# A hybrid decoder step on one Trainium2 core: low parts of the values' weights by VectorE alone, and an end in a written order that leaves GpSimd out

## The chip, the core and the metric

The kernel runs on one core of a Trainium2 chip. The core's engines work side by side, each through its own queue in order: TensorE (PE; its weight loads are shown as PEld), VectorE (DVE), ScalarE (ACT), GpSimd (POOL) and SyncE (SP), which here only starts DMAs. GpSimd and ScalarE can start DMAs too. [...] An engine waits for another by a semaphore. The metric is the device time of one execution in microseconds (us), less is better.

## What is computed

The reference is one layer of a decoder for 512 prompt tokens and 64 sample tokens (8 sequences of 8), 1024 wide, all in fp32. Cut to what matters here:

```python
def hybrid_layer(x, ...):
    u = _rms(x) * g_pre_mix
    proj = u @ w_in                       # z, xbc, dt, q, k, v, gates, og
    ...
    y_ssd = ssd_scan(...)                 # Mamba-2 heads, with carried states
    h_ml = mlstm_scan(q, k, v, ...)       # v: 4 heads of 256
    x = x + _rms(mix) * g_post_mix
    ...                                   # cross attention on a memory, the same frame
    u = _rms(x) * g_pre_ffn
    f = (silu(u @ w_gate) * (u @ w_up)) @ w_down
    x = x + _rms(f) * g_post_ffn
    return x, ...
```

The change touches the weights of v within the first projection, and everything from the last part of `@ w_down` for the first 256 tokens on: the sum of squares of f, its root, the residual, and the store of x.

## The kernel before

Activations are kept with features on the 128 partitions and the 576 tokens along the free axis, in 8 tiles. Tokens are worked in two parts, HALVES: 0 to 255 and 256 to 575.

**Products in two parts.** A weight of fp32 is split into a high part hi (fp32r, a cast on ScalarE) and a low part lo = raw - hi; activations likewise. A product is three matmuls: hi by hi, hi by the activation's low part, lo by hi (`gemm`, L201 to L203). `split_w` (L173 to L189) loads a unit of 128 x 1024 weights into one of two `raw` buffers, casts it into one of three `whi` buffers, and makes `wlo` in two pieces: columns 0 to cut on VectorE (L188), the rest either on GpSimd or, with `acc`, by ScalarE writing -hi (L185) and a DMA from GpSimd's queue that adds the weights from HBM onto it (L186).

**Values.** `gemm_tok` (L756) makes v for one head with the tokens on the partitions: two units of weights, `units[0]` for the first four feature tiles and `units[1]` for the other four. For every 128 tokens it runs 4 x 3 matmuls of 256 columns with the first unit, then 4 x 3 with the second (L775 to L777); for the 64 sample tokens, two forms of matmul per feature tile (L767, L768). L793 calls it for the four heads with `acc`, cut at column 512. The memory's values use the same function without `acc`. This stage lies among the state updates of the SSD scan, which run on GpSimd (L589, L597, L633, L725) and VectorE (L598, L611, L614, L729).

**Order.** Most of the kernel is ordered by a planner, which simulates the program with its own durations and so fixes the order on each engine; `tc.issue_after` adds an edge. From the cross attention's output projection to the gated products the order is written by hand: `at_(p, fn, ...)` puts a step at place p of `plan`, and the steps are issued sorted by p inside `tc.manual_schedule`, for the engines named there.

**The end.** The down projection's last 6 feature tiles are added for tokens 256 to 575 first (`down_chunk`), then for tokens 0 to 255, j = 0 to 7: 18 matmuls each (`down_part`), then `down_evac` (L1860): VectorE adds PSUM onto f2 (L1863), ScalarE squares (L262, L266), VectorE adds the square onto `ssqf` (L267), ScalarE scales f2 by the gain (L1865). Between these, for tokens 256 to 575, come the root (`rstd_cols`, `newton`: sums over partitions by matmul with ones, L226; mean on VectorE, L236; power -0.5 on GpSimd, L237; one Newton step on VectorE, L238 to L240), its rows by transposes (L251) copied by ScalarE (L253), and the residual (`post_add`, VectorE, L1038, L1039) with four stores of 320 KB from SyncE (L1918). `x2` holds x, loaded back from DRAM. Where an order is not written it is the planner's.

`final0` then does tokens 0 to 255, which leave with tokens on the partitions, in four quarters `parts`: 4 transposes of x2 per quarter (L1876) and a copy to SBUF on ScalarE (L1884), the root of `ssqf`, 4 transposes of f2 per quarter, and quarter 0, 1 and 3 on VectorE (L1898: f2 by the root plus x); quarter 2 is scaled on ScalarE (L1895) and added on GpSimd (L1896). SyncE issues the four stores of 256 KB (L1899). PE's order is written here: three quarters of x, the sums of the root, the fourth, then f2. L2020 is the closing of the program: each engine drains, and GpSimd collects and releases the barrier.

Of the kernel before, what the change touches and what calls it, by code (L numbers as in the profile page):

```python
# [116 lines left out]
def build(nc, tc, ctx, I, O):  # L117
# [27 lines left out]
    def B0(name):  # L145
        return pn[0].tile([P, 512], F32, name=name, tag="n0")
# [26 lines left out]
    def split_w(src, n=1024, cut=CUT, acc=False, pool=None, to=None, raw=None):  # L173
        if raw is None:
            raw = wp.tile([P, 1024], F32, name="raw", tag="raw", bufs=2)
        loads.append(S.dma_start(raw[:, :n], src))
        if to:
            split(*to, raw[:, :n])
            return to
        hi, lo = [(pool or wp).tile([P, 1024], F32R, name=k, tag=k, bufs=NWX if pool else 3) for k in ("whi", "wlo")]  # L180
        A.copy(hi[:, :n], raw[:, :n])  # L181
        for e, a, b in ((V, 0, cut), (G, cut, n)):
            if b > a and e is G and acc:

                A.activation(lo[:, a:b], hi[:, a:b].bitcast(F32), AF.Copy, scale=-1.0)  # L185
                G.dma_start(lo[:, a:b], src[:, a:b], accum_op=ALU.add)  # L186
            elif b > a:
                e.tensor_tensor(lo[:, a:b], raw[:, a:b], hi[:, a:b].bitcast(F32), op=ALU.subtract)  # L188
        return hi, lo  # L189
# [30 lines left out]
    def rstd_cols(ssq, chunks, name, d=1024.0, alloc=None):  # L220

        nch = len(chunks)
        ps = (alloc or BP)("ps_ss")
        for j in range(nch):
            for i, t_ in enumerate(ssq):
                ssq_mm.append(mm(ps[:, j:j + 1], t_[:, chunks[j][0]:chunks[j][0] + P], ones, start=i == 0,  # L226
                                 stop=i == len(ssq) - 1, skip_group_check=True))
        return newton(ps[:, :nch], [P, nch], name, d)
# [524 lines left out]
        G.memset(v_[:, :, 256:257], 1.0)  # L753
        G.memset(v_[:, :, 257:258], 0.0)

    def gemm_tok(src, xh_, xl_, chunks, evac, acc=False, units=None):  # L756

        units = units or [split_w(src[:, i, :], acc=acc) for i in range(2)]
        for c0 in range(0, len(chunks), 2):
            ps = GP("ps_v")  # L760
            for c, (t0, n) in enumerate(chunks[c0:c0 + 2]):
                if n == TS:

                    for k in range(KT):
                        hi, lo = units[k // 4]
                        j = (k % 4) * 256
                        mm(ps[:, 0:256], xh_(k, t0, P), hi[:, j:j + 256], start=k == 0, stop=k == KT - 1, skip_group_check=True)  # L767
                        mm(ps[:n, 0:256], xh_(k, t0, n), lo[:, j:j + 256], start=False, stop=k == KT - 1, skip_group_check=True)  # L768
                    break
                for k in range(KT):  # L770
                    hi, lo = units[k // 4]
                    j = (k % 4) * 256
                    ah, al = xh_(k, t0, n), xl_(k, t0, n)
                    o = ps[:n, c * 256:c * 256 + 256]
                    mm(o, ah, hi[:, j:j + 256], start=k == 0, stop=False, skip_group_check=True)  # L775
                    mm(o, al, hi[:, j:j + 256], start=False, stop=False, skip_group_check=True)
                    m = mm(o, ah, lo[:, j:j + 256], start=False, stop=k == KT - 1, skip_group_check=True)  # L777
            evac(c0, ps)
        return m

    def v_evac(h):
        def ev(c, ps):
            if c < 4:
                for i in range(2):
                    A.activation(vt4[:, c + i, h, 0:256], ps[:, 256 * i:256 * i + 256], AF.Copy, scale=rx[:, c + i:c + i + 1])
            else:
                A.copy(vts[:TS, h, 0:256], ps[TS:P, 0:256])
                V.tensor_tensor(vts[:TS, h, 0:256], vts[:TS, h, 0:256], ps[:TS, 0:256], op=ALU.add)
                A.activation(vts[:TS, h, 0:256], vts[:TS, h, 0:256], AF.Copy, scale=rx[:TS, 4:5])
        return ev  # L790

    for h in range(4):
        gemm_tok(I["wv"][h], U, UL, CHUNKS, v_evac(h), True)  # L793


    st = ExitStack()
# [983 lines left out]
    def down_part(c, nk, j, i, ps, w, k0, k1):  # L1780
        t0, n = HALVES[i]
        return gemm(ps, [(*w, nk)], act(hh), act(hl), t0, n, k0, k1)
# [86 lines left out]
    with tc.issue_after(loads[-1].ins):  # L1869
        S.dma_start(x2, x_d)  # L1870

    def final0():

        def rows(src, c, d, ps):
            for j in range(4):
                m = TE.transpose(ps[:, j * P:(j + 1) * P], src[:, 4 * d + j, c * P:(c + 1) * P], ident)  # L1876
            return ps.rearrange("p (j k) -> p j k", j=4), m

        parts = [(c, d) for c in range(2) for d in range(2)]
        xr = [wp.tile([P, 2, 4, P], F32, name="raw", tag="raw", bufs=2) for _ in range(2)]  # L1880
        xt = [xr[i // 2][:, i % 2] for i in range(4)]

        def put(i):
            A.copy(xt[i], rows(x2, *parts[i], (B1 if i == 3 else GP)("ps_xt"))[0])  # L1884

        with tc.manual_schedule(engines={TE.engine}):
            for i in range(3):
                put(i)
            rc = rstd_cols([ssqf], HCHUNKS[0], "pf0", alloc=B0)
            put(3)  # L1890
            ft = [rows(f2, *parts[i], (GP if i == 3 else MP)("ps_ft"))[0] for i in range(4)]
        for i, (c, d) in enumerate(parts):
            if i == 2:
                t = sw[:, 0:512].rearrange("p (j k) -> p j k", j=4)
                A.activation(t, ft[i], AF.Copy, scale=rc[:, c:c + 1])  # L1895
                G.tensor_tensor(xt[i], xt[i], t, op=ALU.add)  # L1896
            else:
                V.scalar_tensor_tensor(xt[i], ft[i], rc[:, c:c + 1], xt[i], op0=ALU.mult, op1=ALU.add)  # L1898
            S.dma_start(O["y0"][c, :, 4 * d:4 * d + 4, :], xt[i])  # L1899


    for n_, j in enumerate(range(8)):
        ps = (MP if n_ % 2 else GP)("ps_dn")[:, :256]
        m = down_part(2, 6, j, 0, ps, w_of(j), 0, 6)
        e = down_evac(n_, j, 0, ps, m)
        if n_ == 0:
            with tc.issue_after(m.ins):
                rc = rstd_cols([ssqf], HCHUNKS[1], "pf1", alloc=B0)
        if n_ == 1:
            with tc.issue_after(m.ins):  # L1910
                rstd_rows(rc, HCHUNKS[1], rb, B0)
        if n_ > 1:
            ks = range(8)[:2] if n_ == 2 else range(8)[n_ - 1:n_] if n_ < 7 else range(6, 8)
            for k in ks:
                with tc.issue_after(e[1].ins):
                    post_add(1, f2, x2, rb, [k], False)
                if k % 2:
                    S.dma_start(O["y1"][:, k - 1:k + 1, :], x2[:, k - 1:k + 1, 256:T])  # L1918
    final0()


def _units(w, kt):
# [102 lines left out]
```

## Time and profile before

| what | value |
|---|---|
| median of 3 runs | 1122.03 us (1121.79 to 1123.79) |
| the profiled execution | 1122.92 us, its span 1121.2 us |
| granted TensorE clock, mean | 0.998 |
| DMA | 178.67 MB, mean 159 GB/s |
| of it from GpSimd's queue (q0) | 39.33 MB |
| loads of the values' weights | 8 x 512 KB, median 5.7 us to landing |
| accumulating DMAs of the values' low parts | 8 x 256 KB, median 6.8 us to landing |
| PE busy in 1107.5 to 1112.0 | 3.43 us of 4.5 |
| PE busy in 1112.0 to 1121.2 | 0.70 us of 9.2 |

The span runs from the first to the last instruction of the profiled execution; some 1.7 us of its time lie around it. Times within the trace count from the span's start. A busy PE is a modelled figure: matmuls overlap, so that a matmul of 256 columns is shown as 0.28 us while the next starts 0.12 us later. Drains and semaphore instructions belong to an engine's sequencer and are not counted as busy; they have rows of their own under the line that issued them.

### The profile page before, as it was taken

The page shows a single profiled execution, that of the slowest core. Times are in us where ns is not written, and L with a number is a line of the kernel's source. Part 1 is how long each engine was busy: PE and PEld are TensorE (multiplying, and loading weights), DVE is VectorE, ACT ScalarE, POOL GpSimd, SP SyncE. Part 2 cuts the span into 40 slices and gives each one's busy share as a digit, 9 for nine tenths or more (in the row PEclk, how much of TensorE's full clock was granted, in tenths as well). Part 3 has the DMA queues.
Part 4 walks back from the last instruction along what each step waited for, and adds up shares of the span by engine and source line. Part 5 has one row for each costly group of instructions (what it writes and reads, how often), then busy time and mean ns, then how long its engine had stood idle before and what let it go on. Part 6 is the DMA issues. An engine that isn't in the chain of part 4 may idle for free.

```text
span 1121.2 us, 21126 instructions
## 1 busy us (share of the span) xinstructions
PE 1100.6 (98%) x8423; PEld 1049.9 (94%) x8423; DVE 703.7 (63%) x1397; ACT 594.3 (53%) x1073; POOL 223.0 (20%) x300
## 2 busy tenths in 40 slices
PE   9999999899999999999999999999999999999996
PEld 8999889798998999999988889999999999999996
DVE  6796765557786775569654455776533665447555
ACT  6877533255563465656454445556435674246543
POOL 1333544313122121000144301101001110011001
PEclk9999999999999999999999999999999999999999
DMA  6685555626564447653567855745535774357532
GB/s 208 159 165 128 134 159 159 174 68 166 146 201 107 129 144 264 226 189 104 167 223 278 282 197 170 253 114 123 141 95 122 171 169 123 94 119 169 123 127 85
DMA packets 56231, 178.67 MB, mean 159 GB/s; under 512 B 6172, under 2 KB 10396, under 8 KB 55620
## 3 DMA queue, kind: packets, MB, share of 16 engines
q1 hardware_dynamic: 41732, 137.99, 37.8%
q0 software_dynamic: 14400, 39.33, 18.2%
q8 instruction: 66, 1.08, 0.4%
q14 instruction: 33, 0.27, 0.1%
HBM read 156.64 MB, written 20.65 MB: 158 GB/s over the span
## 4 chain that ended last, share of the span: by engine, by line
PE 89%; DMA 4%; DVE 2%; ACT 2%; issue 1%; POOL 1%; SPq 0%; DVEq 0%; POOLq 0%; ACTq 0%
PE ps_in L202 6%; PE ps_in L201 6%; PE ps_in L203 6%; PE ps_dn L203 4%; PE ps_dn L201 4%; PE ps_dn L202 4%; PE ps_o L203 3%; PE ps_o L202 3%; PE ps_o L201 3%; PE ps_g L1719 3%; PE ps_g L1720 3%; PE ps_g L1721 3%; PE ps_u L1719 3%; PE ps_u L1720 3%; PE ps_u L1721 3%; PE ps_v L777 2%
## 5 line engine op out<-in xcount | busy, mean ns | idle before, releaser
L181 ACT CAST whi<-raw 128x1024 fp32r<-128x1024 f32 x110 | 114.6, 1045 | 113.6 <-PE ps_dn L202 22.0
L202 PE MATMUL ps_in<-ul,whi 128*128 128x320 f32 (+1 forms) x544 | 164.3, 302 | 0.0
L201 PE MATMUL ps_in<-uh,whi 128*128 128x320 f32 (+1 forms) x544 | 163.9, 301 | 0.0
L203 PE MATMUL ps_in<-uh,wlo 128*128 128x320 f32 (+1 forms) x544 | 163.0, 300 | 0.5 <-DVE wlo L188 0.5
L188 DVE TENSOR_TENSOR wlo<-raw,whi 128x1024 fp32r<-128x1024 f32 (+1 forms) x102 | 102.8, 1009 | 82.0 <-ACT whi L181 81.2
L202 PEld LDWEIGHTS ps_in<-ul,whi 128*128 128x128 f32 x544 | 103.1, 190 | 2.5 <-issue 1.7
L201 PEld LDWEIGHTS ps_in<-uh,whi 128*128 128x128 f32 x544 | 103.1, 190 | 2.2 <-issue 1.3
L203 PEld LDWEIGHTS ps_in<-uh,wlo 128*128 128x128 f32 x544 | 103.1, 190 | 1.8 <-DVE wlo L188 0.7
L203 PE MATMUL ps_dn<-hh,wlo 128*128 128x320 f32 (+1 forms) x280 | 82.3, 296 | 0.8 <-DVE wlo L188 0.8
L201 PE MATMUL ps_dn<-hh,whi 128*128 128x320 f32 (+1 forms) x280 | 81.8, 296 | 0.6 <-ACT whi L181 0.5
L202 PE MATMUL ps_dn<-hl,whi 128*128 128x320 f32 (+1 forms) x280 | 82.0, 294 | 0.0
L203 PEld LDWEIGHTS ps_dn<-hh,wlo 128*128 128x128 f32 x280 | 52.5, 188 | 1.2 <-DVE wlo L188 1.2
L201 PEld LDWEIGHTS ps_dn<-hh,whi 128*128 128x128 f32 x280 | 52.3, 188 | 1.0 <-ACT whi L181 0.7
L202 PEld LDWEIGHTS ps_dn<-hl,whi 128*128 128x128 f32 x280 | 52.9, 189 | 0.0
L186 POOL DMA_DIRECT2D wlo<-win x32 | 27.9, 880 | 95.2 <-ACT wlo L185 89.2
L1719 PE MATMUL ps_u<-b,whi 128*128 128x288 f32 x144 | 42.5, 295 | 0.6 <-ACT ct L1751 0.6
L1720 PE MATMUL ps_u<-b,whi 128*128 128x288 f32 x144 | 42.5, 295 | 0.0
L1719 PE MATMUL ps_g<-b,whi 128*128 128x288 f32 x144 | 42.5, 295 | 0.0
L1720 PE MATMUL ps_g<-b,whi 128*128 128x288 f32 x144 | 42.5, 295 | 0.0
L777 PE MATMUL ps_v<-wlo,uh 128*128 128x256 f32 x128 | 36.5, 288 | 3.8 <-DMA wlo<-wv 3.8
L1671 POOL DMA_DIRECT2D wacc<-wgate x9 | 7.8, 871 | 159.4 <-ACT wacc L1670 147.1
L201 PE MATMUL ps_xo<-qh,whi 128*128 128x288 f32 x128 | 37.7, 300 | 1.0 <-ACT f_xo L1407 1.0
(720 smaller groups left out, 3681.3 us busy)
## 6 DMA issues: line engine op xcount, KB each, us to landing
raw<-win SPq DMA_DIRECT2D x35, 512.0 KB, 3.8
raw<-wout SPq DMA_DIRECT2D x17, 512.0 KB, 3.7
kva<-kc SPq DMA_DIRECT2D x16, 512.0 KB, 6.7
kva<-vc SPq DMA_DIRECT2D x16, 512.0 KB, 6.5
raw<-wdown SPq DMA_DIRECT2D x16, 512.0 KB, 3.6
raw<-wxq SPq DMA_DIRECT2D x13, 512.0 KB, 3.6
raw<-wgate SPq DMA_DIRECT2D x13, 512.0 KB, 3.6
raw<-wup SPq DMA_DIRECT2D x13, 512.0 KB, 5.1
```

The lines of the kernel that those rows point to most:

```text
L181: A.copy(hi[:, :n], raw[:, :n])
L186: G.dma_start(lo[:, a:b], src[:, a:b], accum_op=ALU.add)
L188: e.tensor_tensor(lo[:, a:b], raw[:, a:b], hi[:, a:b].bitcast(F32), op=ALU.subtract)
L201: mm(ps, wh, ah, start=i == 0, stop=False)
L202: mm(ps, wh, al, start=False, stop=False)
L203: m = mm(ps, wl, ah, start=False, stop=i == len(tiles) - 1)
L777: m = mm(o, ah, lo[:, j:j + 256], start=False, stop=k == KT - 1, skip_group_check=True)
L1671: G.dma_start(out, s.src[j, :, c], accum_op=ALU.add)
L1719: mm(ps, wh, b[0][:, k, :], start=start and k == 0, stop=False, skip_group_check=True)
L1720: mm(ps, wh, b[1][:, k, :], start=False, stop=False, skip_group_check=True)
L1721: m = mm(ps, wl, b[0][:, k, :], start=False, stop=k == 3, skip_group_check=True)
```

## The change

In the values' products the parameter `acc` of `gemm_tok` becomes `cut`, and the four heads pass 1024: VectorE makes the whole low part, and no scaling on ScalarE and no DMA on GpSimd's queue are left there. The memory's values are as before.

The end for tokens 0 to 255 is written out with `at_` as one plan over all five engines, in units of one j:
- every j has its 18 matmuls, its add, square and scaling, and the add of its square to `ssqf`, except j = 7, whose square goes into the root's sums as a second term;
- the root takes a square root on ScalarE and a reciprocal on VectorE where GpSimd had the power;
- the residual and stores of tokens 256 to 575 lie at 2.95, 4.1, 5.1 and 6.1, two tiles in one operation;
- the transposes of x2 and their copies lie at 4 to 7.55, all in PSUM bank `n1`;
- behind j = 7: sums, transposes of f2, root, three quarters on VectorE, the last one scaled on ScalarE and added on VectorE;
- the stores of quarters 1 and 3 are issued by ScalarE.

```diff
--- before.py
+++ after.py
@@ -753,9 +753,9 @@
         G.memset(v_[:, :, 256:257], 1.0)
         G.memset(v_[:, :, 257:258], 0.0)
 
-    def gemm_tok(src, xh_, xl_, chunks, evac, acc=False, units=None):
-
-        units = units or [split_w(src[:, i, :], acc=acc) for i in range(2)]
+    def gemm_tok(src, xh_, xl_, chunks, evac, cut=CUT, units=None):
+
+        units = units or [split_w(src[:, i, :], cut=cut) for i in range(2)]
         for c0 in range(0, len(chunks), 2):
             ps = GP("ps_v")
             for c, (t0, n) in enumerate(chunks[c0:c0 + 2]):
@@ -790,7 +790,7 @@
         return ev
 
     for h in range(4):
-        gemm_tok(I["wv"][h], U, UL, CHUNKS, v_evac(h), True)
+        gemm_tok(I["wv"][h], U, UL, CHUNKS, v_evac(h), 1024)
 
 
     st = ExitStack()
@@ -1869,54 +1869,121 @@
     with tc.issue_after(loads[-1].ins):
         S.dma_start(x2, x_d)
 
-    def final0():
-
-        def rows(src, c, d, ps):
-            for j in range(4):
-                m = TE.transpose(ps[:, j * P:(j + 1) * P], src[:, 4 * d + j, c * P:(c + 1) * P], ident)
-            return ps.rearrange("p (j k) -> p j k", j=4), m
-
-        parts = [(c, d) for c in range(2) for d in range(2)]
-        xr = [wp.tile([P, 2, 4, P], F32, name="raw", tag="raw", bufs=2) for _ in range(2)]
-        xt = [xr[i // 2][:, i % 2] for i in range(4)]
-
-        def put(i):
-            A.copy(xt[i], rows(x2, *parts[i], (B1 if i == 3 else GP)("ps_xt"))[0])
-
-        with tc.manual_schedule(engines={TE.engine}):
-            for i in range(3):
-                put(i)
-            rc = rstd_cols([ssqf], HCHUNKS[0], "pf0", alloc=B0)
-            put(3)
-            ft = [rows(f2, *parts[i], (GP if i == 3 else MP)("ps_ft"))[0] for i in range(4)]
-        for i, (c, d) in enumerate(parts):
-            if i == 2:
-                t = sw[:, 0:512].rearrange("p (j k) -> p j k", j=4)
-                A.activation(t, ft[i], AF.Copy, scale=rc[:, c:c + 1])
-                G.tensor_tensor(xt[i], xt[i], t, op=ALU.add)
-            else:
-                V.scalar_tensor_tensor(xt[i], ft[i], rc[:, c:c + 1], xt[i], op0=ALU.mult, op1=ALU.add)
-            S.dma_start(O["y0"][c, :, 4 * d:4 * d + 4, :], xt[i])
-
-
-    for n_, j in enumerate(range(8)):
-        ps = (MP if n_ % 2 else GP)("ps_dn")[:, :256]
-        m = down_part(2, 6, j, 0, ps, w_of(j), 0, 6)
-        e = down_evac(n_, j, 0, ps, m)
-        if n_ == 0:
-            with tc.issue_after(m.ins):
-                rc = rstd_cols([ssqf], HCHUNKS[1], "pf1", alloc=B0)
-        if n_ == 1:
-            with tc.issue_after(m.ins):
-                rstd_rows(rc, HCHUNKS[1], rb, B0)
-        if n_ > 1:
-            ks = range(8)[:2] if n_ == 2 else range(8)[n_ - 1:n_] if n_ < 7 else range(6, 8)
-            for k in ks:
-                with tc.issue_after(e[1].ins):
-                    post_add(1, f2, x2, rb, [k], False)
-                if k % 2:
-                    S.dma_start(O["y1"][:, k - 1:k + 1, :], x2[:, k - 1:k + 1, 256:T])
-    final0()
+
+    plan = []
+    tail, squares = {}, {}
+
+    def root(name, terms, chunks):
+
+        n, ps = len(chunks), B0("ps_ss")
+        for c, (t0, _) in enumerate(chunks):
+            for m, (t_, b) in enumerate(terms):
+                mm(ps[:, c:c + 1], t_[:, t0 - b:t0 - b + P], ones, start=m == 0, stop=m == len(terms) - 1, skip_group_check=True)
+        v, y, a, r = [fp.tile([P, n], F32, name=name + k) for k in ("_v", "_y", "_a", "_r")]
+        tail[name] = v, y, a, r
+        V.tensor_scalar(v, ps[:, :n], 1.0 / 1024.0, EPS, op0=ALU.mult, op1=ALU.add)
+        A.activation(y, v, AF.Sqrt)
+
+    def root_end(name):
+        v, y, a, r = tail[name]
+        V.reciprocal(y, y)
+        V.tensor_tensor(a, y, y, op=ALU.mult)
+        V.scalar_tensor_tensor(a, a, -0.5, v, op0=ALU.mult, op1=ALU.mult)
+        V.scalar_tensor_tensor(r, a, 1.5, y, op0=ALU.add, op1=ALU.mult)
+        tail[name] = r
+
+    def root_rows1():
+        tail["ps"] = ps = B0("ps_rb")
+        for c, (t0, n) in enumerate(HCHUNKS[1]):
+            TE.transpose(ps[:, t0 - 256:t0 - 256 + n], tail["pf1"][:n, c:c + 1].to_broadcast([n, P]), ident[:n, :n])
+
+    def half0(j, k):
+        if k == 0:
+            tail[j] = (MP if j % 2 else GP)("ps_dn")[:, :256]
+        down_part(2, 6, j, 0, tail[j], w_of(j), k, k + 1)
+
+    def evac0(j):
+        fj = f2[:, j, 0:256]
+        V.tensor_tensor(fj, fj, tail[j], op=ALU.add)
+        if j:
+            squares[j] = ph.tile([P, 320], F32, name="sq", tag="sq", bufs=2)[:, :256]
+        A.activation(squares[j] if j else ssqf[:, 0:256], fj, AF.Square)
+        A.activation(fj, fj, AF.Copy, scale=PAR("g_postffn", j))
+
+    def sum0(j):
+        V.tensor_tensor(ssqf[:, 0:256], ssqf[:, 0:256], squares[j], op=ALU.add)
+
+    def resid1(q):
+        o, c = f2[:, 2 * q:2 * q + 2, 256:T], x2[:, 2 * q:2 * q + 2, 256:T]
+        V.tensor_tensor(o, o, rb[:, 256:T].unsqueeze(1).to_broadcast([P, 2, 320]), op=ALU.mult)
+        V.tensor_tensor(c, c, o, op=ALU.add)
+        S.dma_start(O["y1"][:, 2 * q:2 * q + 2, :], c)
+
+    for j in range(8):
+        for k in range(6):
+            at_(j + k / 6, half0, j, k)
+        at_(j + 1.03, evac0, j)
+        if 0 < j < 7:
+            at_(j + 1.45, sum0, j)
+    at_(0.99, root, "pf1", [(ssqf, 0)], HCHUNKS[1])
+    at_(1.9, root_end, "pf1")
+    at_(2.32, root_rows1)
+    at_(2.6, lambda: A.copy(rb[:, 256:T], tail["ps"][:, 0:320]))
+    for q, p in enumerate((2.95, 4.1, 5.1, 6.1)):
+        at_(p, resid1, q)
+
+    parts = [(c, d) for c in range(2) for d in range(2)]
+    xr, xt, ft = [], {}, {}
+
+    def token_rows(src, i, ps):
+        c, d = parts[i]
+        for j in range(4):
+            TE.transpose(ps[:, j * P:(j + 1) * P], src[:, 4 * d + j, c * P:(c + 1) * P], ident)
+        return ps.rearrange("p (j k) -> p j k", j=4)
+
+    def x_rows(i):
+        if i % 2 == 0:
+            xr.append(wp.tile([P, 2, 4, P], F32, name="raw", tag="raw", bufs=2))
+        xt[i] = xr[i // 2][:, i % 2], token_rows(x2, i, B1("ps_xt"))
+
+    def x_copy(i):
+        A.copy(*xt[i])
+
+    def f_rows(i):
+        ft[i] = token_rows(f2, i, (MP if i % 2 else GP)("ps_ft"))
+
+    def last(i):
+        o, rc = xt[i][0], tail["pf0"][:, parts[i][0]:parts[i][0] + 1]
+        V.scalar_tensor_tensor(o, ft[i], rc, o, op0=ALU.mult, op1=ALU.add)
+        store(i)
+
+    def store(i):
+        c, d = parts[i]
+        (A if i in (1, 3) else S).dma_start(O["y0"][c, :, 4 * d:4 * d + 4, :], xt[i][0])
+
+
+    def scaled():
+        tail["s"] = sw[:, 0:512].rearrange("p (j k) -> p j k", j=4)
+        A.activation(tail["s"], ft[3], AF.Copy, scale=tail["pf0"][:, parts[3][0]:parts[3][0] + 1])
+
+    def scaled_add():
+        V.tensor_tensor(xt[3][0], xt[3][0], tail["s"], op=ALU.add)
+        store(3)
+
+    for i in range(4):
+        at_(4.0 + i, x_rows, i)
+        at_(4.55 + i, x_copy, i)
+        at_(8.7 + i / 100, f_rows, i)
+    at_(8.4, lambda: root("pf0", [(ssqf, 0), (squares[7], 0)], HCHUNKS[0]))
+    at_(8.8, root_end, "pf0")
+    at_(9.0, scaled)
+    for i in range(3):
+        at_(9.01 + i / 100, last, i)
+    at_(9.1, scaled_add)
+    plan.sort()
+    with tc.manual_schedule(engines={TE.engine, A.engine, V.engine, G.engine, S.engine}):
+        for _, _, fn in plan:
+            fn()
 
 
 def _units(w, kt):
```

## Prediction

> **What bounds the kernel now.** I read the page's head first, then the core's 20 us windows, to find where TensorE (PE) is not busy.
>
> ```profile
> span 1121.2 us, 21126 instructions
> PE 1100.6 (98%) x8423; PEld 1049.9 (94%) x8423; DVE 703.7 (63%) x1397; ACT 594.3 (53%) x1073; POOL 223.0 (20%) x300
> ...
> 180.00:200.00 20.00, 17.90 (x138) 15.51 (x137) 8.50 (x12) 6.94 (x12) 11.65 (x10) 1.00 0.60 172
> 200.00:220.00 20.00, 18.30 (x137) 15.70 (x135) 12.02 (x21) 7.88 (x14) 8.00 (x6) 1.00 0.53 143
> ...
> 1100.00:1120.00 20.00, 11.63 (x97) 10.91 (x96) 11.95 (x31) 6.65 (x14) 2.07 (x2) 0.94 0.33 119
> ```
>
> PE sets the time: it is idle for 1121.2 - 1100.6 = 20.6 us in all. The columns of a window are its length, then PE, PEld, DVE, ACT and POOL busy, clock, DMA share, GB/s. Two windows in the middle lose 2.10 and 1.70 us, and the last one 8.37 us. The change touches just these two places: the values' projection, and the end. So the sum has two terms.
>
> For the first, PE's timeline; in brackets stands the idle time before an instruction and what ended it:
>
> ```profile
> 199.64 0.39 PE L777 MATMUL ps_v<-wlo,uh 128*128 128x256 f32 x1 [2.10 <-DMA wlo<-wv]
> ...
> 219.66 0.39 PE L777 MATMUL ps_v<-wlo,uh 128*128 128x256 f32 x1 [1.70 <-DMA wlo<-wv]
> ```
>
> All idle time of both windows, 2.10 + 1.70 = 3.8 us, ends with the accumulating DMA that finishes a low part. The chain of waits shows why it is late:
>
> ```profile
> 185.61 3.83 POOL h L725 x2
> ...
> 190.68 0.60 POOL hs L597
> ...
> 191.66 7.93 DMA wlo<-wv
> 199.64 0.39 PE ps_v L777
> 200.26 0.12 PE ps_v L777
> ```
>
> The DMA is issued from GpSimd's queue, behind two state updates (L725), and takes 7.93 us from issue to landing.
>
> For the end, the chain of waits from the last matmul of the down projection (PE leaves it at 1107.47), and line L2020, the program's closing barrier:
>
> ```profile
> 1107.47 0.45 PE ps_xt L1876 x4
> ...
> 1107.95 1.07 ACT raw L1884 x2
> 1109.02 0.32 ACT sq L266
> ...
> 1109.37 0.44 DVE ssqf L267
> ...
> 1109.85 0.60 PE ps_ss L226 x4
> ...
> 1110.95 1.76 PE ps_ft L1876 x16
> ...
> L2020 POOLq EVENT_SEMAPHORE x4: 17/17/17, 1120.4 to 1121.1; - x4
> L2020 POOLq DRAIN x3: 46/93/6939, 1113.4 to 1120.9; - x3
> L2020 SPq DRAIN x3: 7/7/7, 1117.8 to 1120.6; - x3
> ...
> SPq L2020 <- PEq L2020: 3.2, 2, 2.7
> ```
>
> Two things are to be seen. The last square waits behind two copies of x's transposes on ScalarE. And the end is not set by the stores: SyncE has seen them land and drains at 1117.8, then sits 2.7 us. GpSimd's drain, 6939 ns long, begins at 1113.4 behind its last add and ends at 1120.37, and GpSimd's first semaphore of the barrier follows at 1120.4. Behind it come 0.8 us that stay.
>
> **Values' weights.** For 8 units (4 heads x 2), the scaling of half a unit on ScalarE (0.63 us) and the 256 KB accumulating DMA go; VectorE subtracts 1024 columns where it subtracted 512.
>
> ```profile
> L185 ACT ACTIVATE wlo<-whi x12: 616/630/632, 149.8 to 257.4; 128x512 fp32r<-128x512 f32 x12
> ...
> L188 DVE TENSOR_TENSOR wlo<-raw,whi 128x512 fp32r<-128x512 f32 x12 | 11.5, 958 | 8.3 <-ACT whi L181 8.3
> ...
> L188 DVE TENSOR_TENSOR wlo<-raw,whi x12: 676/692/1721, 152.4 to 257.4; 128x512 fp32r<-128x512 f32 x12
> ...
> L188 DVE TENSOR_TENSOR wlo<-raw,whi 128x1024 fp32r<-128x1024 f32 x52 | 63.5, 1222 | 42.1 <-ACT whi L181 41.9
> L181 ACT CAST whi<-raw 128x1024 fp32r<-128x1024 f32 x10 | 10.3, 1046 | 10.0 <-PE ps_in L202 4.6 <-PE ps_v L776 4.5 <-PE ps_v L767 0.9
> ```
>
> The columns of a grouped row are busy time, mean ns and idle time before; a row with a colon gives minimum, median and maximum in ns. L188's first two rows are this stage's, its third the whole kernel's. The wide subtract costs 1.22 us on the mean, about 1.5 us here (958 ns for the half width; an estimate), at worst 2 x 1.72 = 3.44. VectorE gets some 8 x 0.5 = 4 us more, in windows where it is busy 8.5 and 12.0 of 20 us: free. What counts is how fast a slot of whi turns round. With three slots, the second unit of a head can be cast only when the head before has read its own first unit for the last time. From there PE has 8 matmuls of that head and 12 of the next before it needs the new unit: 20 x 0.12 = 2.4 us (0.12 is one matmul's share in the chain above). Cast plus subtract is 1.05 + 1.5 + 0.1 = 2.65, late by 0.25 at three heads, 0.75 in all; at best (1.22) nothing. Other stages' matmuls stand between, so I take half, 0.4. The DMA path needed 1.05 + 0.63 + 7.9 and GpSimd's turn. What is late next is the cast itself. Gain: 3.8 - 0.4 = **3.4 us**, between 0 and 4.
>
> The planner orders these engines from simulated times, so its order from here up to the written order near 660 us can change. No row prices this; I bound it by 3.8 us, the one loss that its present order has here, on the bad side, and 1 us on the good.
>
> The slow subtracts lie beside GpSimd's state updates (L725). [...]
>
> **End.** Let T be PE's end of the down projection.
> - T moves later. The 16 transposes of x2, of which 12 stood in the shadow behind T, go between its matmuls, where PE has no idle time: 4 x 0.45 = 1.8 us. The copies and y1's adds (two per pair of tiles) go beside the matmuls: VectorE then has per tile its two adds of 256 columns (0.41 and 0.44) and two operations of 640 columns, 2 x 0.9 by L1038's 3.6 us for 8 of half the width: 2.65 us, against PE's 18 x 0.12 + 0.45 = 2.6. That is cover without reserve for four tiles, and PE waits for none of these adds there; they are no longer in the last tile, and y1's four stores leave SyncE's queue before T.
> - Behind T, from these rows:
>
> ```profile
> 1107.59 0.41 DVE L1863 TENSOR_TENSOR f_ffn<-f_ffn,ps_dn 128x256 f32<-128x256 f32 x1
> ...
> 1110.92 0.15 DVE L236 TENSOR_SCALAR pf_v<-ps_ss 128x2 f32<-128x2 f32 x1
> ...
> 1112.73 2.07 DVE L1898 SCALAR_TENSOR_TENSOR raw<-ps_ft,pf_r,raw 128x512 f32<-128x512 f32 x3
> ...
> 1111.21 0.81 POOL L237 TENSOR_TENSOR pf_y<-pf_v,c 128x2 f32<-128x2 f32 x1 [14.26 <-DVE pf_v L236]
> 1113.47 1.26 POOL L1896 TENSOR_TENSOR raw<-raw,sw 128x512 f32<-128x512 f32 x1 [1.45 <-ACT sw L1895]
> ...
> 1095.00 0.73 PE L226 MATMUL ps_ss<-c,ssqf 128*128 128x1 f32 x6
> ...
> L933 ACT ACTIVATE exs<-ps_mx 128x1 f32<-128x1 f32 x2 | 0.3, 162 | 0.3 <-PE ps_mx L931 0.3
> ...
> 1113.51 2.08 SPq L1899 DMA_DIRECT2D o_y<-raw  x4
> ...
> L1038 DVE TENSOR_TENSOR f_ffn<-f_ffn,pf_rb 128x320 f32<-128x320 f32 x8 | 3.6, 484 | 0.0
> ...
> L1671 POOL DMA_DIRECT2D wlo<-wup x1: 862/862/862, 1050.2 to 1050.2; - x1
> ```
>
> The add ends at T + 0.53; the square, with nothing ahead of it, at 0.98; the sums are twice as many rows (8), of which 2 can run early, so 0.73 for 6: 1.8; mean 2.0. The square root on ScalarE, on two columns, has its nearest row in L933's 0.16, with its handover 0.2: 2.2 (GpSimd's power: 0.81). A reciprocal and three small operations at 0.2 each: 3.0. The transposes of f2 need 1.76 from 1.7 and stay ahead of their readers. Three multiply-adds 2.07, then the fourth quarter's add on VectorE, 0.69 as L188's half width: 5.9 (before, GpSimd's ran beside: 1114.73 - 1107.47 = 7.3). The last store is issued at once on ScalarE's queue instead of behind another on SyncE's. From the fourth issue's start (1115.59 - 0.44) to SyncE's drain at 1117.8 it is 2.65: 8.6. With GpSimd free since its last DMA issue at 1050 (L1671), its drain is over long before, so the barrier follows: 8.6 + 0.05 + 0.8 = T + 9.4 against 1121.2 - 1107.5 = 13.7. That is -4.3, with the 1.8 of T **-2.5 us**. Of it 2.6 is the drain; all the rest together is even.
>
> Bounds: transposes 1.7 to 2.4 (a changeover each); the drain's gain 0 to 2.6; square root 0 to 1.3 more.
>
> Sum: 3.4 + 2.5 = 5.9 us. The profiled execution took 1122.92, span 1121.2; the runs' median is 1122.03, 0.9 below it. Taken from the median: **1116.1 us**.
>
> **Rivals.**
> 1. The planner's order, or the slower turn of whi, eats the first term; the second stays: 1122.0 - 2.5 = 1119.5. For it: the waits stand at 98% busy, where small shifts show. Against: a subtract that the planner can place is nearer to its simulation than a DMA behind GpSimd's queue.
> 2. GpSimd's drain is long or late whatever ran on it before, so that 2.6 us stay: 1118.7. For it: no row shows a GpSimd that comes idle to the kernel's end. Against: L2020's other two drains of GpSimd, with nothing ahead of them, take 93 and 46 ns; the long one is behind work.
> 3. A table load for the square root on the last chain.
>
> ```profile
> L688 ACT ACT_TABLE_LOAD x1: 1283/1283/1283, 122.8 to 122.8; - x1
> ...
> L262 ACT ACTIVATE ssqg<-xs x4: 417/444/472, 261.5 to 300.4; 128x256 f32<-128x256 f32 x2, 128x320 f32<-128x320 f32 x2
> ```
>
> This load is Exp's, at 122.8; squares run behind it, from 261.5 on, without one of their own. So I expect one load at the first root, beside matmuls, and none at the second. If squares did need one, 1283 ns come onto the chain: 1117.4. [...]
> 4. Slower: the low part now waits in VectorE's own queue.
>
> ```profile
> 227.44 2.16 DVE L611 SCALAR_TENSOR_TENSOR lm<-ps_l,ncum,c 128x128 f32<-128x128 f32 x8 [1.12 <-PE ps_l L608]
> ```
>
> Behind such a group of eight and beside L725, a handover takes 1.05 + 2.16 + 3.44 = 6.65, 4.25 over the cover, 12.8 us at three heads: 12.8 - 3.8 - 2.5 = +6.5, 1128.5. It decides from 2.8 us per handover. Against: the planner knows the subtract and can put it ahead; the median subtract shows no such place.
>
> **How the numbers follow.** Forecast 0.57, rival 1 0.20, rival 2 0.10, rival 3 0.07, rival 4 0.06. The forecast's own range is 1114.5 to 1117.8. 0.2% is 2.2 us, about what a measurement of this kernel tells from no change, so faster begins below 1119.8. Rival 1 gives back between 3 and 5 us: 0.06 of it faster, 0.14 within. Faster 0.57 + 0.06 + 0.10 + 0.07 = 0.80, same 0.14, slower 0.06. The range of 8 in 10 runs from 1113.0 (the planner 1 us better, tail bounds at their good ends) to 1120.6, most of rival 1.
>
> **What would show it.** L777 without a wait for a DMA and PE busy over 19.5 us in both middle windows: first term right. L2020's GpSimd drain short or begun near 1050, and SyncE's wait in the barrier under 0.3 us: second term right. L1884's copies before T, the sums' matmuls within 1.2 us of T, one new table load near 1093. PE idle under a VectorE wlo in the values' stage, or new PE waits between 260 and 660, would make it wrong, as would a tile of the end in which PE waits for f2's adds.

## The result and the profile after

| kernel | median | runs | ratio to before (95%) |
|---|---|---|---|
| before | 1122.91 us (1121.79 to 1124.12) | 4 | |
| changed | 1116.89 us (1115.92 to 1117.10) | 4 | 0.9943 (0.9931 to 0.9955) |

The change takes 6.0 us off the median, where 5.9 were forecast (1122.0 to 1116.1); by the ratio it is 6.4. A second measurement gave the same ratio, 0.9943 (0.9931 to 0.9955).

The head of the page, the two middle windows and the rows of the closing barrier (now line L2087: minimum, median and maximum in ns, then first and last start), all of the changed kernel. The last row is SyncE's waiting in the barrier: in all, number of waits, longest:

```profile
span 1115.3 us, 21087 instructions
PE 1101.1 (99%) x8427; PEld 1050.9 (94%) x8427; DVE 709.2 (64%) x1391; ACT 591.5 (53%) x1068; POOL 214.7 (19%) x289
...
180.00:200.00 20.00, 20.00 (x156) 17.75 (x155) 10.04 (x13) 6.72 (x12) 9.94 (x8) 1.00 0.39 133
200.00:220.00 20.00, 20.00 (x158) 17.13 (x158) 15.24 (x24) 7.02 (x13) 6.83 (x5) 1.00 0.42 153
...
L2087 POOLq EVENT_SEMAPHORE  x4: 17/17/17, 1114.3 to 1115.2; - x4
L2087 POOLq DRAIN  x3: 46/93/8038, 1046.8 to 1114.8; - x3
L2087 SPq DRAIN  x3: 7/7/7, 1114.2 to 1114.5; - x3
...
SPq L2087 <- PEq L2087: 0.9, 2, 0.8
```

PE is busy for the whole of both windows, in which it had lost 3.8 us. GpSimd's long drain is not gone (8038 ns, longer than before), but it begins at 1046.8 and is over at 1054.8. The barrier's first semaphore on GpSimd comes at 1114.3, within 0.1 us of SyncE's drain at 1114.2. So SyncE's first wait there, which was 2.7 us, is 0.15 (0.9 less 0.74); its second, in the closing half of the barrier, is 0.74 where it was 0.45. And from the last matmul of the down projection (T, 1105.98) the chain of waits is:

```profile
1103.77 0.44 PE ps_xt L1941 x4
...
1106.02 0.43 DVE f_ffn L1907
...
1106.47 0.42 ACT sq L1910
...
1106.94 0.84 PE ps_ss L1881 x6
...
1107.81 0.17 DVE pf_v L1884
...
1108.00 0.21 ACT pf_y L1885
...
1108.83 0.17 DVE pf_r L1892
...
1109.11 1.41 DVE raw L1957 x2
...
1111.18 0.60 DVE raw L1970
```

To see where PE gains and loses, I paired each matmul of a trace with the same one of the profile of before (the n-th of its form and tiles) and took the median difference of their starts around a place. That is the table on which most of what follows rests; negative is earlier than before. In kernels whose order differs from before's, the figure at 260 moves by 0.2 to 0.4 us with how many matmuls around the place are taken. "Dips" counts stretches between 180 and 400 in which the granted clock falls to half.

| kernel | 150 | 260 | 700 | 720 | 1060 | T | span's end - T | dips |
|---|---|---|---|---|---|---|---|---|
| before | 0 | 0 | 0 | 0 | 0 | 1107.47 | 13.69 | 0 |
| changed | -0.19 | -4.58 | -4.72 | -3.61 | -3.38 | 1105.98 | 9.34 | 0 |
| changed, again | 0.83 | -3.56 | -4.16 | -3.98 | -3.75 | 1105.68 | 9.35 | 0 |
| values only | -0.05 | -4.43 | -4.92 | -4.74 | -4.65 | 1102.86 | 13.03 | 0 |
| end only | 0.14 | 0.60 | 0.44 | 1.33 | 1.91 | 1111.29 | 9.06 | 1 |
| old end without GpSimd | -0.34 | 1.11 | 0.31 | 1.40 | 1.40 | 1108.90 | 10.99 | 1 |
| old end, quarter 2 on VectorE | -0.48 | 1.80 | 2.26 | 2.26 | 3.35 | 1110.83 | 11.14 | 1 |
| changed + small GpSimd copy | 0.19 | -4.23 | -4.70 | -3.64 | -3.41 | 1105.97 | 12.25 | 0 |
| changed + GpSimd's add | -0.65 | -5.07 | -4.56 | -3.46 | -3.22 | 1106.20 | 11.73 | 0 |
| low parts half by GpSimd | 0.43 | -1.36 | 1.11 | 1.15 | 1.40 | 1110.80 | 9.04 | 1 |
| x in the gap | 0.26 | -4.14 | -4.74 | -4.37 | -2.85 | 1105.69 | 9.34 | 0 |
| late cast | -0.19 | -4.60 | -5.33 | -5.29 | -4.73 | 1104.66 | 9.35 | 0 |
| both | -0.60 | -5.03 | -5.16 | -5.13 | -4.20 | 1104.34 | 9.35 | 0 |
| end only + small copy | -0.32 | 0.62 | 0.82 | 0.86 | 1.11 | 1110.50 | 12.47 | 1 |

### The profile page after: what moved, and what is told of

Same layout as the page of the kernel before. It is cut to its first block, busy times and chain, and to the rows that moved or that the text cites. A ratio compares the mean times of both kernels' runs of the same rounds, so it can differ in the third digit from the quotient of the medians.

```text
span 1115.3 us, 21087 instructions
## 1 busy us (share of the span) xinstructions
PE 1101.1 (99%) x8427; PEld 1050.9 (94%) x8427; DVE 709.2 (64%) x1391; ACT 591.5 (53%) x1068; POOL 214.7 (19%) x289
## 4 chain that ended last, share of the span: by engine, by line
PE 90%; DMA 4%; DVE 3%; ACT 2%; issue 1%; SPq 0%; DVEq 0%; POOL 0%; ACTq 0%; POOLq 0%
PE ps_in L201 6%; PE ps_in L202 6%; PE ps_in L203 6%; PE ps_dn L201 4%; PE ps_dn L203 4%; PE ps_dn L202 4%; PE ps_o L201 3%; PE ps_o L203 3%; PE ps_o L202 3%; PE ps_g L1719 3%; PE ps_g L1720 3%; PE ps_g L1721 3%; PE ps_u L1719 3%; PE ps_u L1720 3%; PE ps_u L1721 3%; PE ps_v L777 2%
## 5 line engine op out<-in xcount | busy, mean ns | idle before, releaser
L188 DVE TENSOR_TENSOR wlo<-raw,whi 128x1024 fp32r<-128x1024 f32 (+1 forms) x102 | 107.8, 1059 | 83.3 <-ACT whi L181 82.6
L201 PE MATMUL ps_xq<-u2h,whi 128*128 128x320 f32 (+1 forms) x128 | 38.2, 303 | 0.0
```

Source lines behind the costliest of these rows:

```text
L201: mm(ps, wh, ah, start=i == 0, stop=False)
```

## Experiments

The theory: the first term is the landing of the accumulating DMA, which PE waited for; the second is GpSimd's closing drain, counted from its last work. Rivals: the planner's new order is the first gain; the rearranged tail is the second, and the drain indifferent. In each cut of an edit, `...` marks what is left out.

### The drain: four kernels

**Old end without GpSimd.** The kernel before, in its own order; only GpSimd's work in the end goes:

```diff
+    def power(y, v, p, w):
+        pows.append(G.tensor_tensor(y, v, C32("nhalf")[:p, :w], op=ALU.pow))
...
+    def root(y, v, p, w):
+        A.activation(y, v, AF.Sqrt)
+        V.reciprocal(y, y)
...
-        pows.append(G.tensor_tensor(y, v, C32("nhalf")[:shape[0], :w], op=ALU.pow))
+        (root if name in ("pf0", "pf1") else power)(y, v, shape[0], w)
...
-            if i == 2:
-                t = sw[:, 0:512].rearrange("p (j k) -> p j k", j=4)
-                A.activation(t, ft[i], AF.Copy, scale=rc[:, c:c + 1])
-                G.tensor_tensor(xt[i], xt[i], t, op=ALU.add)
-            else:
-                V.scalar_tensor_tensor(xt[i], ft[i], rc[:, c:c + 1], xt[i], op0=ALU.mult, op1=ALU.add)
+            V.scalar_tensor_tensor(xt[i], ft[i], rc[:, c:c + 1], xt[i], op0=ALU.mult, op1=ALU.add)
```

> The kernel before, in its own order, with only GpSimd's two kinds of work taken out of the end: square root on ScalarE and reciprocal on VectorE for the power, and quarter 2 as a fourth multiply-add on VectorE. Theory (GpSimd's closing drain, 5.64 us behind its last work, sets the end): the drain is over long before the stores, VectorE's four operations end near 1115.4, SyncE drains near 1118.0, so 2.2 to 2.5 us faster than before, the whole of the end's gain without its new order. Rival (the rearranged tail is the gain, a drain comes late whatever ran): within 0.4 us of before, GpSimd's drain still ends near 1120.

**Quarter 2 on VectorE** is the last part of that edit alone (quarter 2 as a multiply-add on VectorE); the power stays on GpSimd.

> The kernel before with only quarter 2 moved to VectorE; the power stays on GpSimd and is its last work, near 1112.0. Theory (a drain of about 5.6 us counted from the last work): drain over near 1117.7, about when the stores have landed, so 1.9 to 2.4 us faster than before. If the drain's length hangs on the size of the last operation, it is over far earlier and the time is that of the kernel without GpSimd. Rival (drain late whatever ran): no change.

**Small GpSimd copy**, in the changed kernel:

```diff
     at_(9.1, scaled_add)
+    at_(9.2, lambda: G.tensor_copy(gt[:, 0, 0:2], xt[3][0][:, 0, 0:2]))
```

> The changed kernel with one GpSimd copy of 128x2 added, which reads quarter 3 behind VectorE's last add and which nothing waits for. Theory: the copy ends near T + 6.0 (1112), a drain of 5.6 us follows to 1117.6, and the kernel ends 2.8 to 3.3 us later than the changed one. Rival (the drain is indifferent, or its length comes from the size of the work behind which it stands): less than 0.5 us.

**Quarter 3's add on GpSimd**, in the changed kernel:

```diff
-        V.tensor_tensor(xt[3][0], xt[3][0], tail["s"], op=ALU.add)
+        G.tensor_tensor(xt[3][0], xt[3][0], tail["s"], op=ALU.add)
```

> The changed kernel with quarter 3's add on GpSimd (1.26 us in the kernel before) instead of VectorE (0.68). Theory: GpSimd's add ends near T + 5.2 (1111.2), the drain near 1116.9, the end 2.2 to 2.8 us later than the changed kernel, although the last store is issued earlier. Rival (only the chain of data counts): 0.3 to 0.5 us faster, because VectorE's last add of 0.68 goes.

Measured, five rounds on one chip with 22 runs of before (median 1123.81): without GpSimd 1121.54, 0.9980 (0.9970 to 0.9989); quarter 2 on VectorE 1120.85, 0.9973 (0.9962 to 0.9984); small copy 1119.25, 0.9964 (0.9952 to 0.9977); GpSimd's add 1118.35, 0.9957 (0.9944 to 0.9970). The times of the first two scatter with what happens in the values' stage (below), so the stretch behind T decides: 10.99 and 11.14 against 13.69 before, that is -2.70 and -2.55 us; 12.25 and 11.73 against 9.34 after, +2.91 and +2.39. All four lie in what the theory gave or 0.2 us beyond it, none near the rivals. On the clock, by the ratios to before (0.9943 for the changed kernel), they are -2.2, -3.0, +2.4 and +1.6 us: the first is in its range, the other three lie 0.4 to 0.6 us outside theirs, which is less than the intervals leave open (over 1 us to a side); there too none is near its rival. GpSimd's timeline and the barrier's rows, of the small copy first, then of GpSimd's add, then of quarter 2 on VectorE (the row with SPq and PEq is again SyncE's waiting in the barrier):

```profile
1111.83 0.18 POOL L1983 COPY gt<-raw 128x2 f32<-128x2 f32 x1 [64.19 <-DVE raw L1970]
...
L2088 POOLq DRAIN  x3: 93/193/5192, 1111.8 to 1117.8; - x3
L2088 SPq DRAIN  x3: 7/7/7, 1114.2 to 1117.3; - x3
...
SPq L2088 <- PEq L2088: 3.9, 2, 2.9
```

```profile
1110.60 1.26 POOL L1970 TENSOR_TENSOR raw<-raw,sw 128x512 f32<-128x512 f32 x1 [62.78 <-ACT sw L1967]
...
L2087 POOLq DRAIN  x3: 46/93/6287, 1110.6 to 1117.7; - x3
```

```profile
1114.57 0.81 POOL L237 TENSOR_TENSOR pf_y<-pf_v,c 128x2 f32<-128x2 f32 x1 [14.26 <-DVE pf_v L236]
...
L2015 POOLq DRAIN  x3: 46/102/6477, 1114.5 to 1121.7; - x3
L2015 SPq DRAIN  x3: 7/7/7, 1121.1 to 1121.4; - x3
```

The row of a drain starts when the engine begins to wait, so its end is what counts: start plus longest. A copy of two columns, which nothing reads, ends at 1112.0 and its drain at 1117.0; SyncE had drained at 1114.2 and sits 2.9 us. The add ends at 1111.86, its drain at 1116.85. So in both the drain ends 4.99 us behind GpSimd's last operation, be that a copy of 128x2 or an add of 128x512. In the third kernel the power ends at 1115.38 and the drain at 1121.0, level with SyncE at 1121.1: there it just no longer shows.

### The two parts by themselves

**Values only** is the kernel before with the first two hunks of the change; **end only** is the changed kernel without them.

> The kernel before with only the values' part of the change: VectorE makes the whole low part, the end is the old one. Theory (the two waits for the accumulating DMA go): no wait of L777 for a DMA, PE at the same matmul 4.5 to 5 us earlier than before at 300 us, 3.4 to 4.9 us earlier at 1060 (1.1 us less where a load of wup lands late near 705, which the drain experiments showed to come and go from execution to execution), behind T the old 13.7; time 3.4 to 4.9 us below before. Rival (the planner's new order and the slower whi turn eat it): under 2 us below before.

> The changed kernel with the values' low parts as before (half of each by the accumulating DMA): the end alone. Theory: the waits of L777 for the DMA are back (1.7 to 5 us in 180 to 260), T is 1.9 us later against the same place at 1060, behind T it is 9.3 in place of 13.7; time 2.5 us below before, between 2.0 and 3.0. Rival (the two parts of the change only work together, since the planner's order is one): off by over 1 us from the sum, that is e1 and e2 together not 6.0 us below before.

Measured (five rounds, one chip, before 1123.29): values only 1117.92, 0.9954 (0.9942 to 0.9966); end only 1120.93, 0.9980 (0.9970 to 0.9991). Those are -5.2 us, 0.3 more than the theory's range, and -2.2 us. Their sum, 7.4, is 1.0 more than both together by the same kind of ratio (6.4), and 1.4 more than the 6.0 of the medians that the expectation named; by its words that is the rival's sign. Of the excess 0.7 has a cause, shown below; the other 0.3 to 0.7 is within the intervals, each 1.2 to 1.4 us to a side. Values only has the changed kernel's order on PE (the first 8144 matmuls are the same) and no wait at L777; end only has before's order and its two waits back. So in these kernels the removal of the DMA and the new order come together: PE's order departs from before's at 166 us, and no kernel tried has the old order without the DMA. That the removal is the gain rests on the two waits, which are gone in every kernel without the DMA. The table gives the price of the transposes ahead of T: from 1060 to T the changed kernel loses 3.38 - 1.49 = 1.89 us, end only 3.82 - 1.91 = 1.91, values only nothing.

Values only also ends 0.66 us sooner behind T than before (13.03 against 13.69), with the same end. Its drain shows why: it ended 4.99 us behind GpSimd's last add, before's 5.64. The two kernels with a late drain that lack the 8 accumulating DMAs (92 DMAs issued by GpSimd in all) have 4.99 as well, the two that have them (100) 5.64. In values only this shortens the end; in the changed kernel the drain no longer counts, so the parts share this 0.66. One more kernel, the end alone with the small copy, told that apart:

> The end alone (the values' low parts half by the accumulating DMA, as before) with the small GpSimd copy behind the last add. GpSimd's closing drain ended 5.64 us behind its last operation in the two profiles whose GpSimd had issued 100 DMAs (before, and quarter 2 on VectorE), and 4.99 to 5.00 us behind it in the three with 92 (values only, small copy, quarter 3 on GpSimd). If the DMAs issued set its length: 5.6 us here, with 100 DMAs. If the form of the end sets it: 5.0 us, as with the small copy before.

Its copy and its barrier:

```profile
1116.36 0.18 POOL L1983 COPY gt<-raw 128x2 f32<-128x2 f32 x1 [64.20 <-DVE raw L1970]
...
L2088 POOLq DRAIN  x3: 46/102/5844, 1116.3 to 1122.7; - x3
```

1116.34 + 5.84 is 1122.18, 5.64 us behind the copy's end at 1116.54: the longer drain goes with the eight accumulating DMAs, not with the form of the end. Whether their number, their bytes or their kind counts was not separated. One run of it took 1124.74 beside 1124.23 for before; it says nothing on the time.

### Low parts half by GpSimd

The changed kernel with `gemm_tok(I["wv"][h], U, UL, CHUNKS, v_evac(h), 512)`: GpSimd subtracts the second half of each low part, so there is no DMA, but a turn in GpSimd's queue.

> The changed kernel with the values' low parts made half by VectorE and half by a subtract on GpSimd: no accumulating DMA, but still a turn in GpSimd's queue. If the landing of the DMA (7.9 us) is what PE waited for, little of a wait is left: the time of the changed kernel, within 0.8 us. If the turn behind the state updates (3.83 us for two) is what counts, L777 waits for GpSimd's low part, 1 to 4 us in all between 180 and 260, and the kernel is that much slower than the changed one. If the planner's order is the gain, PE is where it was before at 300 us.

Measured 1120.82, 0.9982 (0.9972 to 0.9992), 4.4 us slower than the changed kernel by the ratios. No wait at L777 is left, as the first theory said, yet the time is nearly that of before: none of the three came out as stated. PE's order is a third one, and PE waits elsewhere. Its windows beside the changed kernel's:

```profile
200.00:260.00 60.00, 58.37 (x483) 52.11 (x482) 33.24 (x73) 24.17 (x43) 18.92 (x17) 1.00 0.43 120
260.00:400.00 140.00, 138.28 (x1004) 128.93 (x1003) 106.23 (x290) 70.87 (x155) 31.39 (x44) 0.99 0.49 137
...
257.75 1.09 PE L619 MATMUL ps_yi<-lm,xdt 128*64 128x128 f32 x16 [1.63 <-DVE lm L614]
...
357.82 0.64 PE L914 MATMUL ps_nh<-c,qpad 128*32 128x257 f32 x8 [1.72 <-DMA c<-c]
```

```profile
200.00:260.00 60.00, 60.00 (x502) 54.96 (x502) 39.39 (x81) 26.13 (x48) 16.42 (x17) 1.00 0.44 132
260.00:400.00 140.00, 140.00 (x1020) 129.70 (x1020) 108.71 (x293) 75.00 (x160) 29.84 (x40) 1.00 0.48 135
```

The sum of this kernel's two waits is 3.35 us, and behind the second the granted clock falls (0.64 in 358 to 360, 0.51 in 360 to 362). So what rival 1 of the prediction fears, a gain eaten by new waits elsewhere, can happen in this stage; the change as made escaped it. How much of the loss is GpSimd's longer work (18.92 against 16.42 us) and how much the order was not taken apart.

### Three variants of the changed kernel

**X in the gap**: two quarters of x's transposes behind T.

```diff
-        xt[i] = xr[i // 2][:, i % 2], token_rows(x2, i, B1("ps_xt"))
+        xt[i] = xr[i // 2][:, i % 2], token_rows(x2, i, (GP if i == 3 else B1)("ps_xt"))
...
-        at_(4.0 + i, x_rows, i)
-        at_(4.55 + i, x_copy, i)
+        at_((4.0, 5.0, 8.1, 8.2)[i], x_rows, i)
+        at_((4.55, 5.55, 8.3, 8.5)[i], x_copy, i)
```

> The changed kernel with quarters 2 and 3 of x's transposes behind the last matmul of the down projection (one of them in another PSUM bank, the copies between ScalarE's scaling, square root and last scaling), where PE waits 0.84 us for the last square. Theory (that gap is free, and the 16 transposes ahead of T cost 0.44 us per four): T 0.88 us earlier, behind T 9.3 to 9.5, time 0.7 to 0.9 us below the changed kernel. Rival (the two copies of 0.55 us on ScalarE delay the square root and the last scaling): behind T 10 or more, no gain.

Measured 1115.47, 0.9931 (0.9919 to 0.9943). PE's and ScalarE's timeline behind T, with the gap filled:

```profile
1105.53 1.04 PE L1941 MATMUL ps_xt<-c,x 128*128 128x128 f32 x8
1106.40 0.28 PE L1881 MATMUL ps_ss<-c,ssqf 128*128 128x1 f32 x2
1106.65 0.38 PE L1881 MATMUL ps_ss<-c,sq 128*128 128x1 f32 x2
...
1107.05 0.56 ACT L1950 COPY raw<-ps_xt 128x512 f32<-128x512 f32 x1
1107.71 0.20 ACT L1885 ACTIVATE pf_y<-pf_v 128x2 f32<-128x2 f32 x1
1107.82 0.57 ACT L1950 COPY raw<-ps_xt 128x512 f32<-128x512 f32 x1
```

From 1060 to T it loses 1.07 us instead of 1.89, and behind T it takes the same 9.34: 0.82 us, as expected. On the clock it stands at 0.9931 against 0.9943, with intervals that overlap.

**Late cast**, for the 1.1 us that the changed kernel's table row loses between 700 and 720. There ScalarE's queue holds a cast that waits for a load of `wup`, and the last square before a root stands behind it; PE waits in turn (ScalarE's row, then PE's):

```profile
704.81 1.05 ACT L1436 CAST whi<-raw 128x1024 fp32r<-128x1024 f32 x1 [1.33 <-DMA raw<-wup]
...
707.90 0.83 PE L1465 MATMUL ps_ss<-c,ssqxo 128*128 128x1 f32 x6 [0.81 <-DVE ssqxo L1541]
```

```diff
     for n_, (key, p) in enumerate(order):
...
-        at_(order[n_ - 2][1] + 0.01 if n_ > 1 else -1, load, key, src)
+        p = 8.03 if key == ("u", 1) else p
+        at_((8.03 if n_ == 9 else order[n_ - 2][1]) + 0.01 if n_ > 1 else -1, load, key, src)
```

**Both** joins the two. The changed kernel ran beside them.

> The changed kernel once more, beside the next two on the same chip. Theory of the clock (a PE wait of about 2 us in the values' stage halves the granted clock for some 3.4 us in part of the executions, which costs 1.7 us on top of the wait; the changed kernel has no such wait): its executions lie within 2 us of each other at a mean clock of 0.998 or more, while before spreads over 4 us and more with clocks down to 0.995. Rival (the spread is the chip's, whatever the kernel): both spread alike.

> The changed kernel with the cast of up-projection unit 1 moved from 7.6 to 8.03 of the written order, behind the last evacuation of xo, and the load that follows it moved along. Theory (what is given back near 707 is ScalarE waiting in its queue for this unit's load, with the last square of ssqxo behind it): no PE wait at L1465, PE at the same matmul about 4.7 us earlier than before at 720 as at 700, 0.5 to 1.1 us faster than the changed kernel on the median. Rival (the loads themselves are late there, and PE waits for them a little later): PE loses the same 1 us within the next 50 us, no gain.

> The changed kernel with both: two quarters of x's transposes behind the last matmul, and the late cast. If the two gains add: 1.3 to 2.0 us below the changed kernel, near 1115. If the cast's gain is not there: 0.8 us below it, as with the transposes alone.

Measured (five rounds, before 1122.73): changed 1115.94, 0.9943 (0.9931 to 0.9955); late cast 1115.91, 0.9940 (0.9928 to 0.9953); both 1115.27, 0.9937 (0.9923 to 0.9951). The late cast loses nothing between 700 and 720 (-5.33 to -5.29) and gains nothing in time. The loss is no property of the change: the changed kernel lost only 0.2 there this time, while end only and the old end without GpSimd, which have the old values' stage, lose 0.9 and 1.1. It comes and goes from execution to execution with the landing of that load: in the five traces in which the cast waits 1.10 to 1.33 us for it, PE waits 0.59 to 0.83; where the cast waits 0.58 or less, PE does not wait at all. So the edit's gain is unclear. The same holds for both: 0.7 us below the changed kernel on the medians, as the transposes alone should bring, but inside the intervals. Of the versions tried, both and x in the gap are the fastest by their medians; that they beat the changed kernel is shown in the trace for the gap, and not by the clock. As for the clock theory of the changed kernel's second measurement: its five runs lie within 1.6 us at a mean granted clock of 0.998 or 0.999, while before's nine, run beside them, spread over 3.8 us with clocks down to 0.996. That is the theory's side, with before spreading a little less than it said.

## Why the prediction came out right

**First term (3.4 forecast).** Its mechanism held: the waits for the DMA are gone, and the part alone brings the gain. Its size in this profile, 3.4 at 1060, is a coincidence of errors that cancel.
- The waits were sized by the idle column, 2.10 + 1.70. The starts of the matmuls around them tell what they cost:

```profile
197.26 0.28 PE L767 MATMUL ps_v<-whi,uh 128*128 128x256 f32 x1
199.64 0.39 PE L777 MATMUL ps_v<-wlo,uh 128*128 128x256 f32 x1 [2.10 <-DMA wlo<-wv]
```

  From 197.26 to 199.64 it is 2.38 where 0.12 is usual: 2.26; the other comes to 1.98 - 0.12 = 1.86 the same way. That is 4.1, not 3.8, because the 0.28 that a matmul is shown busy overlaps the next one in a stream. PE gains 4.2 to 4.4 between 150 and 260 by the table's way of counting, so smaller differences add 0.3 at most.
- The slower turn of whi (0.4) did not show: no PE wait under a low part. The wide subtract took 1.21 us alone (1.5 was the estimate), but 2.42 and 2.96 beside GpSimd's state updates (the first pair below is one of 2.42 and one of 1.21, the second one of 2.42 and one of 2.96):

```profile
188.27 3.55 DVE L188 TENSOR_TENSOR wlo<-raw,whi 128x1024 fp32r<-128x1024 f32 x2 [3.59 <-ACT whi L181]
206.89 5.29 DVE L188 TENSOR_TENSOR wlo<-raw,whi 128x1024 fp32r<-128x1024 f32 x2
...
185.76 3.84 POOL L725 TENSOR_TENSOR h<-h,decs 128x1024 f32<-128x1024 f32 x2
...
206.28 4.81 POOL L725 TENSOR_TENSOR h<-h,decs 128x1024 f32<-128x1024 f32 x2
```

  GpSimd's pair of updates took 3.84 us beside the first of these and 4.81 beside the second. No matmul that reads a low part waited in these windows.
- The 1.1 us between 700 and 720, which the prediction did not foresee, are given back in some executions of any of these kernels.

**The median hides one thing more**, which the profile of before did not show. In all four other traces of kernels that still have the accumulating DMA, one of the two waits for it is followed by a fall of the granted clock. PE's wait and the 2 us windows around it, of the kernel with quarter 2 on VectorE (the clock is the third figure from the end):

```profile
218.98 0.38 PE L777 MATMUL ps_v<-wlo,uh 128*128 128x256 f32 x1 [1.93 <-DMA wlo<-wv]
...
216.00:218.00 2.00, 1.06 (x10) 0.85 (x7) 1.66 (x3) 0.00 (x0) 0.00 (x0) 1.00 1.01 222
218.00:220.00 2.00, 1.02 (x7) 1.02 (x8) 0.00 (x0) 0.00 (x0) 0.00 (x0) 0.94 1.08 299
220.00:222.00 2.00, 2.00 (x10) 1.81 (x9) 0.69 (x1) 0.00 (x0) 0.00 (x0) 0.50 0.50 198
222.00:224.00 2.00, 2.00 (x15) 1.87 (x15) 0.69 (x1) 0.00 (x0) 0.00 (x0) 0.70 0.15 61
```

At half clock stand 0.24 + 2.0 + 1.2 = 3.4 us. If the clock alone set PE's pace, half of that, 1.7 us, would be lost on top of the wait; the starts of the matmuls, 0.21 apart there in place of 0.12, give 1.5 in each of the four traces. The traces with the whole low part on VectorE have neither the wait nor the dip. Runs without a trace agree in step: of the 22 of before, 11 with a mean clock of 0.998 or 0.999 have a median of 1122.1, 8 with 0.996 or 0.997 one of 1124.0, and 3 with 0.995 one of 1125.8. The mean clock sorts the runs only roughly, since it also holds a fall at the kernel's end (to 0.50 from 1118.0 on in before and from 1114.0 on in the changed kernel): two traces with a dip in this stage show 0.998, as before's without one does. So it is argued rather than shown that on the median the first term is larger than in the profiled execution (values only: -5.2 us). By it the forecast, which took the profile's gain off a median of 1122.03, was right partly by luck: that median, of three runs, held few dips, and with the fourth run before's median is 1122.91.

**Second term (2.5 forecast).** Here step and size held one by one. T came 1.89 later for the 16 transposes (1.8). Behind T: square ended at T + 0.91 (0.98), mean at 1.99 (2.0), square root at 2.2 (2.2), root at 3.0 (3.0), last add at 5.8 (5.9), SyncE's drain at 8.2 (8.6), end at 9.34 (9.4). Of the 0.4 that SyncE was sooner, 0.2 was given back in the barrier: 1.03 us lie behind GpSimd's first semaphore, where 0.8 were to stay. "Of it 2.6 is the drain; all the rest together is even": taking GpSimd out of the old end brought 2.70 with nothing else rearranged, and 9.34 + 1.89 = 11.23 against that kernel's 10.99 leaves a loss of 0.2 for all the rest. So the written order of the end gained nothing of its own: leaving GpSimd out of the old end is the whole second term. VectorE kept up in the last tiles: PE is busy for all 16.0 us from 1090 to 1106.

**Rivals.** 1 (the order eats the first term) did not happen here; with the half on GpSimd new waits did eat it. 2 (a drain late anyway) fell: it began at 1046.8. 3 (a table load on the last chain) fell; the one new load is at the first root, as predicted, though at 1087.5 and not near 1093:

```profile
L1885 ACT ACT_TABLE_LOAD  x1: 1283/1283/1283, 1087.5 to 1087.5; - x1
```

ScalarE's row before it ends at 1087.48 and the square root starts at 1088.80, so the load costs 1.3 us there.

4 (the low part late in VectorE's queue) fell: the subtracts are doubled in the worst places and still in time.

## What to carry to other kernels

Look at which engine's drain is the last one to reach the closing barrier: here a GpSimd copy of 128x2 in the last microseconds ended the kernel 2.9 us later than its stores would have. Size a wait of PE by the starts of the matmuls on both sides of it, and look at the granted clock in the microseconds behind it, in several executions. An edit that clears one wait in a planned stretch may move the order, so run each part by itself and compare matmul by matmul.

## What was not expected of the hardware

- GpSimd's closing drain ended 4.99 us behind its last operation in three kernels where GpSimd had issued 92 DMAs, and 5.64 in three with 100. Where a DMA was its last work, it ended 7.0 to 8.1 us behind the issue of that DMA; counted from its landing that is 3.8 us in the six traces with 92 DMAs (in the changed kernel landing at 1051.0, the drain's end at 1054.8) and 4.1 in the two with 100. Why it takes that long is open.
- Behind four of the ten waits for the accumulating DMA, of 1.79 to 1.93 us, PE's granted clock fell to half for 3.4 us; the other six, of 1.03 to 2.10, passed without. In the kernel with GpSimd's half it fell for 3.4 us behind a wait of 1.72 (0.64, then 0.51, in the two windows from 358 to 362). So the length of a wait alone does not tell whether the clock falls; what decides it was not shown.
- Where GpSimd had nothing left to do in the end, its drain was longer (7.8 to 9.0 us) and cost the end nothing: in the changed kernel it ran from 1046.8 to 1054.8, beside other work.
